# A two-level Strassen matmul with GELU: staging, transposes, split operands and the last outputs rescheduled

## The chip, the core and the metric

One core of a Trainium2 chip (trn2). The metric is the device time of one execution in microseconds (us). Single executions of one kernel spread by several us here. All runs told here count as fast runs (granted clock 0.993 to 1.0 over a whole run). Engines: PE is TensorE (matmul), PEld its weight loads, DVE is VectorE, ACT is ScalarE, POOL is GpSimd, which issues the loads, and SP is SyncE, which issues the stores. PSUM is the memory in which PE accumulates its results.

## The reference

```python
def setup_inputs():
    m, k, n = 4096, 4096, 4096
    return {"a": np.random.randn(m, k).astype(np.float32), "b": np.random.randn(k, n).astype(np.float32)}

def reference(a, b):
    x = np.matmul(a, b)
    return 0.5 * x * (1 + np.tanh(np.sqrt(2 / np.pi) * (x + 0.044715 * x**3)))
```

## The kernel before

A and B are each cut in four quarters. The output is made in 16 blocks ("groups", numbered 0 to 15; four row blocks of A times four column blocks of B), each of which is one tile in every quarter of the output. Seven Strassen products M1 to M7 make a block; block 0 begins with eight plain products, and in blocks 10 to 15 some of the seven are themselves cut by a second Strassen level ("split"). Work is laid out in steps: one step is a quarter of one product, 16 matmuls with 512 columns, 3.45 us. VectorE makes the operand sums (`aS` from A, `bS` from B), the transposes of A (`aT`) and most of the adds of results. ScalarE copies products out of PSUM that are needed again (M5 into `m` or `m5`, M7 into the four buffers `x7`). `bR` is B as loaded; `k_M` and `k_split` are operands of B kept in DRAM, and `bK` is such an operand fetched back; `accX` and `accY` are PSUM.

```python
PRODUCTS = [
    ("M3", "Y", "11", ("12", "22", 1)),          # name, PSUM chain, operand of A, operand of B
    ("M5", "X", ("11", "12", -1), "22"),
    ("M7", "X", ("12", "22", -1), ("21", "22", 1)),
    ("M1", "X", ("11", "22", -1), ("11", "22", -1)),
    ...
]
```

A comes as float32, is cast by the load into one of two `stage` buffers, is transposed by VectorE from there, and is then weighed (squared and summed, for a check of the input's range) by ScalarE in place. The buffer is free for the next load when the weighing is done:

```python
for (quad, h), n in zip(halves, turns(gi)):                 # n: the step of the transpose
    at_step(max(n - LOAD_AHEAD, free_at.pop(0)), load, (load_half, (mb, quad, h)))
    free_at.append(n + 5)
    at_step(n, turn_half, mb, quad, h)
    for x in range(4):                                      # weighed over four steps
        at_step(n + 1 + x, weigh_rows, mb, quad, h, ...)
```

The split products need combined operands of B that are made once, stored to DRAM and fetched for each block. `MAKES` says when: block, product number, step, column block of B, product. Each entry makes five operands, one per step, in the ring `bS` of three buffers, which the sums share:

```python
def make_split(gi, nb, name, p):
    ...
    t = pool.tile([P, 4 * NC], F16, name="bS", tag="bS", bufs=AHEAD + 1)      # AHEAD is 2
    take(t..., o[2], quarter_b(blocks, o[0]), quarter_b(blocks, o[1]))        # VectorE
    keep_operand((nb, "split", s0, k // 2), k % 2, t[:, :])                   # store to DRAM
```

The last block's last output quarter was added up on VectorE, passed through GELU on ScalarE and stored:

```python
elif name == "M6":
    y = post.pop(("x1", i))
    tt(y, X, y, ALU.add)          # VectorE: PSUM + SBUF
    flush()
    waiting.append((gi, i, 1, 1, y, y))   # then ScalarE, then one store of 256 KB
```

## Time and profile before

| | before |
|---|---|
| device time, first 3 runs | 1571.35, 1573.3, 1575.03 us |
| profiled execution | 1571.53 us, span 1570.0 us |
| PE busy | 1547.9 us, 99% of the span |
| VectorE / ScalarE busy | 73% / 38% |
| PE's waits in total | 15.4 us |
| last matmul to the end | 6.65 us |

While its matmuls stay the same, a kernel whose PE is 99% busy can only be improved in the few holes. How the page, PE's waits and its timeline are read for this is shown in the prediction. One more view belongs with them: VectorE's own timeline in block 9, ahead of PE's longest wait (2.79 us, ending at 955.48). Columns: start, duration, engine, line, operation, out<-in, shapes, and in brackets the idle time before it and what ended it.

```profile
937.35 1.22 DVE L933 TENSOR_TENSOR bS<-bK 128x2048 f16<-128x2048 f16 x1
942.29 1.23 DVE L933 TENSOR_TENSOR bS<-bK 128x2048 f16<-128x2048 f16 x1 [3.73 <-DMA k_split<-bS]
...
953.06 1.23 DVE L933 TENSOR_TENSOR bS<-bK 128x2048 f16<-128x2048 f16 x1 [2.92 <-DMA k_split<-bS]
954.20 1.22 DVE L933 TENSOR_TENSOR aS<-aT 128x2048 f16<-128x2048 f16 x1
```

VectorE stands still for 3.73 and 2.92 us (and for 0.85 us in the part left out) until a store of an earlier split operand has landed. The sum `aS` that PE is waiting for stands behind it in VectorE's order, and PE starts 0.06 us after that sum ends (954.20 + 1.22 = 955.42).

### The profile page before, as it was taken

To read this page: it belongs to the slowest core of one execution; us is meant where nothing else is said; L and a number is where in the kernel's file an instruction comes from. 1 tells how busy PE (TensorE), PEld (TensorE's weight loads), DVE (VectorE), ACT (ScalarE), POOL (GpSimd) and SP (SyncE) were. 2 spreads that over 40 slices of the span, in tenths; PEclk is the share of its full clock that TensorE was granted. 3 is DMA by queue.
4 is the path that set the end of the run, shared out by engine and by line. 5 is a ranking of instruction groups with operands and counts; after the bars stand their busy time and mean duration, and the time that the engine had idled before them with its cause. 6 is when DMAs were issued, how large, how long until landed. Compare 5 with 4: busy or idle time off the path is not lost. (4 is left out here: it accounts for less than half of the span.)

```text
span 1570.0 us, 22246 instructions
## 1 busy us (share of the span) xinstructions
PE 1547.9 (99%) x8110; PEld 794.1 (51%) x8110; DVE 1139.6 (73%) x1357; ACT 600.8 (38%) x1322; POOL 462.5 (29%) x830
## 2 busy tenths in 40 slices
PE   9999999999999999999999999999999999999998
PEld 4444444444444444444444443554746457677674
DVE  1598888889778886765557647878749677776774
ACT  5446555465643642211554211121355523232232
POOL 7664433431124311122231222221333312132230
PEclk9999999999999999999999999999999999999999
DMA  9999999994789987799998989898999958688692
GB/s 176 183 224 294 269 304 273 286 216 81 188 220 298 292 299 283 278 416 328 277 283 233 411 317 345 307 414 272 279 263 315 351 156 306 237 283 308 234 332 108
DMA packets 202790, 429.41 MB, mean 274 GB/s; under 512 B 20400, under 2 KB 102320, under 8 KB 200624
## 3 DMA queue, kind: packets, MB, share of 16 engines
q0 software_dynamic: 141472, 265.34, 65.6%
q1 hardware_dynamic: 61200, 162.56, 27.1%
q8 instruction: 66, 1.08, 0.3%
q14 instruction: 52, 0.43, 0.1%
HBM read 340.79 MB, written 162.53 MB: 321 GB/s over the span
## 5 line engine op out<-in xcount | busy, mean ns | idle before, releaser
L468 PEld LDWEIGHTS <-aS 128*128 128x128 f16 x4192 | 410.2, 98 | 510.4 <-issue 7.9
L468 PE MATMUL accX<-bK,aS 128*128 128x512 f16 x1536 | 336.0, 380 | 3.3 <-DVE aS L933 3.3
L933 DVE TENSOR_TENSOR aS<-aT 128x2048 f16<-128x2048 f16 x182 | 217.1, 1219 | 94.7 <-PE accX L468 70.6
L468 PEld LDWEIGHTS <-aT 128*128 128x128 f16 x1600 | 156.6, 98 | 189.2 <-issue 1.4
L919 POOL DMA_DIRECT2D bK<-k_M x236 | 124.8, 534 | 401.5 <-PE accX L468 119.3
L257 POOL DMA_DIRECT2D bR<-in_b_dram x320 | 173.1, 543 | 210.5 <-DMA bR<-in_b_dram 98.2
L271 ACT ACTIVATE stage<-stage 128x512 f16<-128x512 f16 (+1 forms) x320 | 169.5, 532 | 141.0 <-DVE aT L221 108.8
L468 PE MATMUL accY<-bK,aS 128*128 128x512 f16 x896 | 195.0, 379 | 2.2 <-DVE aS L933 1.2
L612 ACT ACTIVATE x<-x 128x512 f32<-128x512 f32 x128 | 78.3, 628 | 251.8 <-DVE x L621 251.7
L468 PE MATMUL accX<-bS,aS 128*128 128x512 f16 x704 | 155.1, 382 | 4.1 <-DVE aS L430 2.5
L430 DVE TENSOR_TENSOR aS<-aT 128x2048 f16<-128x2048 f16 (+1 forms) x112 | 134.0, 1201 | 25.8 <-PE accX L468 14.6
L550 PEld LDWEIGHTS <-aS 128*128 128x128 f16 x1440 | 140.9, 98 | 23.1 <-issue 1.1
L430 DVE TENSOR_TENSOR bS<-bR 128x2048 f16<-128x2048 f16 x110 | 133.5, 1218 | 18.6 <-PE accX L468 13.6
L311 ACT ACTIVATE square<-bR 128x1024 bf16<-128x1024 f16 x120 | 123.1, 1048 | 42.7 <-DVE energy L621 42.0
L257 POOL DMA_DIRECT2D stage<-in_a_dram x144 | 84.5, 593 | 178.8 <-ACT stage L271 106.4
L221 DVE STREAM_TRANSPOSE aT<-stage 128x1024 uint32<-128x1024 uint32 (+1 forms) x61 | 76.0, 1278 | 80.0 <-DMA stage<-in_a_dram 69.5
L579 ACT COPY x<-accX 128x512 f32<-128x512 f32 x116 | 67.8, 586 | 173.0 <-PE accX L468 172.7
L933 DVE TENSOR_TENSOR bS<-bK 128x2048 f16<-128x2048 f16 x70 | 84.3, 1219 | 27.1 <-DMA k_split<-bS 26.9
L621 DVE TENSOR_TENSOR x<-accY,x 128x512 f32<-128x512 f32 x116 | 77.2, 688 | 30.1 <-ACT y L612 20.3
L468 PE MATMUL accY<-bK,aT 128*128 128x512 f16 x448 | 97.8, 379 | 0.0
L468 PE MATMUL accX<-bK,aT 128*128 128x512 f16 x448 | 97.8, 379 | 0.0
L579 ACT COPY m<-accX 128x512 f32<-128x512 f32 x76 | 43.2, 581 | 119.8 <-PE accX L468 95.1
(70 smaller groups left out, 1518.4 us busy)
## 6 DMA issues: line engine op xcount, KB each, us to landing
bK<-k_M POOLq DMA_DIRECT2D x272, 512.0 KB, 10.1
bK<-k_split POOLq DMA_DIRECT2D x90, 512.0 KB, 6.7
bR<-in_b_dram POOLq DMA_DIRECT2D x320, 128.0 KB, 7.4
k_M<-bS SPq DMA_DIRECT2D x80, 512.0 KB, 6.5
k_split<-bS SPq DMA_DIRECT2D x70, 512.0 KB, 7.1
out_dram<-y SPq DMA_DIRECT2D x128, 256.0 KB, 6.3
out_dram<-x SPq DMA_DIRECT2D x128, 256.0 KB, 7.3
stage<-in_a_dram POOLq DMA_DIRECT2D x112, 256.0 KB, 8.4
```

Source lines behind the costliest of these rows:

```text
L221: nc.vector.transpose(dst[:, :, x, :], src)
L257: nc.gpsimd.dma_start(out=dst, in_=src)
L271: nc.scalar.activation(src, src, ACT.Square, accum_out=dst)
L311: nc.scalar.activation(t[:, :], src, ACT.Square)
L430: nc.vector.tensor_tensor(out=x, in0=y, in1=z, op=ALU.add if o[2] > 0 else ALU.subtract)
L468: nc.tensor.matmul(acc[:, :], sa[:, j // 2, i * P : (i + 1) * P, j % 2], sb[:, j, :], start=start and j == 0, stop=stop and j == 3, skip_g ...
L550: nc.tensor.matmul(banks[chain, i][:, :] if wide else out, sa[:, j // 2, r * P : (r + 1) * P, j % 2], sb[:, : NC] if wide else sb[:, j * N ...
L579: nc.scalar.copy(out=t[:, :], in_=src[:, :])
L612: nc.scalar.activation(y[:, :], src[:, :], ACT.Gelu_apprx_tanh)
L621: nc.vector.tensor_tensor(out=o[:, :], in0=x[:, :], in1=y[:, :], op=op)
L919: nc.gpsimd.dma_start(out=dst, in_=kept_unit(*key[1:])[:, x * w : (x + 1) * w])
L933: nc.vector.tensor_tensor(out=t, in0=y, in1=z, op=ALU.add if op > 0 else ALU.subtract)
```

## The change

Its intent: fill PE's holes, each by its own means. The diff, cut to its core:

```diff
-MAKES = ( (6,1,0,1,"M3"), (6,2,1,1,"M5"), (6,3,2,3,"M3"), (6,4,2,3,"M5"), (7,1,3,0,"M2"),
-          (8,2,3,2,"M3"), (8,4,0,2,"M5"), (8,5,3,2,"M1"), (9,2,0,0,"M3"), (9,2,2,0,"M5"),
-          (9,4,2,3,"M1"), (9,5,3,3,"M2"), (10,2,2,2,"M2"), (10,4,0,0,"M1") )
+MAKES = ( (6,0,1,0,"M3"), (6,1,1,1,"M3"), (6,2,1,1,"M5"), (6,3,2,3,"M3"), (7,0,1,2,"M1"),
+          (7,5,3,0,"M2"), (8,2,3,2,"M3"), (8,4,0,2,"M5"), (8,5,3,0,"M5"), (9,1,1,2,"M2"),
+          (9,2,2,3,"M5"), (9,4,0,3,"M1"), (9,5,3,3,"M2"), (10,4,0,0,"M1") )
-SUM_AHEAD = 3      SPLIT_AHEAD = 8      FETCH_AHEAD = 8      LOAD_AHEAD = 7
+SUM_AHEAD = 5      SPLIT_AHEAD = 6      FETCH_AHEAD = 9      LOAD_AHEAD = 9
+RAW_LOAD_AHEAD = 8
+WEIGH_STEPS = 2                       # of the first blocks; the later ones stay at 4
-TURNS = ((2,2), (3,2), (4,2), (5,0), (6,2), (7,3), (9,1), (10,2))
-RAW_TURNS = ((2,2), (3,2), (5,2), (6,1), (7,1), (8,1), (10,1), (11,1))
+TURNS = ((2,2), (3,2), (4,2), (5,0), (6,2), (7,2), (10,1), (10,3))
+RAW_TURNS = ((2,3), (3,3), (5,2), (6,1), (7,1), (8,1), (11,0), (11,0))
-TWO_GROUPS = [x // 2 for x in range(16)] + [8 + 2 * x for x in range(16)]
+TWO_GROUPS = (0,0,1,1,2,2,3,3,4,4,4,4,5,5,5,5,5,7,10,12,14,16,18,18,20,20,24,26,27,27,28,29)
+THIRD = ("22", 1)                     # A22's second half of block 0: four x7 tiles
...
-    (14, "T11_1 W11_1 B11_1a A22_1 B11_1b"),  (16, "T12_1 W12_1:0-4"),  (17, "W12_1:4-16 A21_1"),
+    (14, "T11_1 W11_1 A22_1 B11_1"),          (16, "T12_1"),            (17, "A21_1"),
...  # A22 weighed at steps 18 to 21, A12 at 34 to 49 (before: A12 at 16 and 17, A22 at 34 to 49)
     elif name == "M1":
         m1, x7 = keep("m5", X, 2), post["x7", i]
         tt(x7, x7, m1, ALU.add)
+        if gi == len(groups) - 1:
+            x1 = post.pop(("x1", i))
+            tt(X, X, x1, ALU.add)
...
+    elif gi == len(groups) - 1:       # M6 of the last block
+        flush()
+        if i < RT - 1:
+            emit(gi, i, 1, 1, new_y(), X)
+            return
+        ...
+        for x, queue in enumerate((nc.sync, nc.scalar)):
+            y = new_y()
+            nc.scalar.activation(y[:, :w], X[:, x * w : (x + 1) * w], ACT.Gelu_apprx_tanh)
+            queue.dma_start(out=out[...], in_=y[:, :w])
...
-                at(gi, s, 2 * c, keep_raw, nb, name, ob, c)
+                at(gi, s + 2 * (gi == 1 and name == "M5"), 2 * c, keep_raw, nb, name, ob, c)
```

More of the change, by code (lines that the diff above doesn't have):

```diff
@@ L69 @@
 MAKES = (
-    (6, 1, 0, 1, "M3"),
+    (6, 0, 1, 0, "M3"),
+    (6, 1, 1, 1, "M3"),
     (6, 2, 1, 1, "M5"),
     (6, 3, 2, 3, "M3"),
-    (6, 4, 2, 3, "M5"),
-    (7, 1, 3, 0, "M2"),
+    (7, 0, 1, 2, "M1"),
+    (7, 5, 3, 0, "M2"),
     (8, 2, 3, 2, "M3"),
     (8, 4, 0, 2, "M5"),
-    (8, 5, 3, 2, "M1"),
-    (9, 2, 0, 0, "M3"),
-    (9, 2, 2, 0, "M5"),
-    (9, 4, 2, 3, "M1"),
+    (8, 5, 3, 0, "M5"),
+    (9, 1, 1, 2, "M2"),
+    (9, 2, 2, 3, "M5"),
+    (9, 4, 0, 3, "M1"),
     (9, 5, 3, 3, "M2"),
-    (10, 2, 2, 2, "M2"),
     (10, 4, 0, 0, "M1"),
@@ L86 @@
 STAY_AHEAD = 19
-SUM_AHEAD = 3
+SUM_AHEAD = 5
 BLOCK_AHEAD = 12
-SPLIT_AHEAD = 8
-FETCH_AHEAD = 8
+SPLIT_AHEAD = 6
+FETCH_AHEAD = 9
 SPLITS = {M3_M5: (10, 11, 12, 13, 14, 15), M2_M1: (13, 14, 15)}
-LOAD_AHEAD = 7
-TURNS = ((2, 2), (3, 2), (4, 2), (5, 0), (6, 2), (7, 3), (9, 1), (10, 2))
-RAW_TURNS = ((2, 2), (3, 2), (5, 2), (6, 1), (7, 1), (8, 1), (10, 1), (11, 1))
+RAW_LOAD_AHEAD = 8
+WEIGH_STEPS = 2
+LOAD_AHEAD = 9
+TURNS = ((2, 2), (3, 2), (4, 2), (5, 0), (6, 2), (7, 2), (10, 1), (10, 3))
+RAW_TURNS = ((2, 3), (3, 3), (5, 2), (6, 1), (7, 1), (8, 1), (11, 0), (11, 0))
 PLAIN = [
@@ L104 @@
 N_PLAIN = 2 * len(PLAIN)
-TWO_GROUPS = [x // 2 for x in range(16)] + [8 + 2 * x for x in range(16)]
+TWO_GROUPS = (0, 0, 1, 1, 2, 2, 3, 3, 4, 4, 4, 4, 5, 5, 5, 5, 5, 7, 10, 12, 14, 16, 18, 18, 20, 20, 24, 26, 27, 27, 28, 29)
 C21_FIRST = (0, 5, QPH - 1)
+THIRD = ("22", 1)
 N_WARM = 46
@@ L199, in load_a @@
         x0 = (ih * MH + mb * TM) // Q + x
+        if (quad, c) == THIRD:
+            tiles = staged[mb, quad, c] = staged.get((mb, quad, c), [])
+            ts = []
+            for i in range(x // (NX // RT), (x + n) // (NX // RT)):
+                t = pool.tile([P, NC], F32, name="x7", tag="x7", bufs=RT).bitcast(F16)
+                tiles.append(t.rearrange("p (x r) -> p x r", r=RUN))
+                ts += [
+                    (
+                        tiles[i][g * Q : (g + 1) * Q, :, :],
+                        a_v[kh, g, :, x0 - x + i * NX // RT : x0 - x + (i + 1) * NX // RT, c * RUN : (c + 1) * RUN],
+                    )
+                    for g in range(4)
+                ]
+            return ts
         if not h:
@@ L215, in turn_a @@
         if mb:
-            src = staged[mb, quad, h].rearrange("p x (c r) -> p c x r", c=CH)[:, c]
-        else:
-            src = staged[mb, quad, c][:, x, :]
-        src = src.bitcast(U32).rearrange("p mb (jj q) -> p jj mb q", q=Q)
+            parts = [(x, staged[mb, quad, h].rearrange("p x (c r) -> p c x r", c=CH)[:, c])]
+        elif (quad, c) == THIRD:
+            n = NX // RT
+            parts = [
+                (slice(i * n, (i + 1) * n), staged[mb, quad, c][i]) for i in range(x.start // n, x.stop // n)
+            ]
+        else:
+            parts = [(x, staged[mb, quad, c][:, x, :])]
         dst = a_tiles[mb, quad, c].bitcast(U32).rearrange("p jj (mb q) -> p jj mb q", q=Q)
-        nc.vector.transpose(dst[:, :, x, :], src)
+        for x, src in parts:
+            src = src.bitcast(U32).rearrange("p mb (jj q) -> p jj mb q", q=Q)
+            nc.vector.transpose(dst[:, :, x, :], src)
     def load_half(mb, quad, h):
@@ L292, in weigh_first @@
             k = ((kh * CH + c) * 2 + ih) * NX + x
-            weigh_row(stats["a"][:, k : k + 1], staged[0, quad, c][:, x, :])
+            n = NX // RT
+            row = staged[0, quad, c][x // n][:, x % n, :] if (quad, c) == THIRD else staged[0, quad, c][:, x, :]
+            weigh_row(stats["a"][:, k : k + 1], row)
     def weigh_first_half():
@@ L682, in settle_fresh @@
             waiting.append((gi, i, 0, 0, y, y))
-        elif name == "M6":
+        elif gi == len(groups) - 1:
[3 more added lines that the diff above has]
+                return
+            mb, nb = groups[gi]
+            r0, c0, w = MH + mb * TM + i * P, NH + nb * NC, NC // 2
+            for x, queue in enumerate((nc.sync, nc.scalar)):
+                y = new_y()
+                nc.scalar.activation(y[:, :w], X[:, x * w : (x + 1) * w], ACT.Gelu_apprx_tanh)
+                queue.dma_start(out=out[r0 : r0 + P, c0 + x * w : c0 + (x + 1) * w], in_=y[:, :w])
+        else:
             y = post.pop(("x1", i))
@@ L727, in half_path @@
         (9, "T22_0 W22_0 A12_1+B21_1a B21_1b"),
-        (14, "T11_1 W11_1 B11_1a A22_1 B11_1b"),
-        (16, "T12_1 W12_1:0-4"),
-        (17, "W12_1:4-16 A21_1"),
-        (18, "S2 S3 T22_1"),
-        (23, "T21_1"),
-        (34, "W22_1:0-1"),
-        (35, "W22_1:1-2"),
-        (36, "W22_1:2-3"),
-        (37, "W22_1:3-4"),
-        (38, "W22_1:4-5"),
-        (39, "W22_1:5-6"),
-        (40, "W22_1:6-7"),
-        (41, "W22_1:7-8"),
-        (42, "W22_1:8-9"),
-        (43, "W22_1:9-10"),
-        (44, "W22_1:10-11"),
-        (45, "W22_1:11-12"),
-        (46, "W22_1:12-13"),
-        (47, "W22_1:13-14"),
-        (48, "W22_1:14-15"),
-        (49, "W22_1:15-16"),
+        (14, "T11_1 W11_1 A22_1 B11_1"),
+        (16, "T12_1"),
+        (17, "A21_1"),
+        (18, "S2 S3 T22_1 W22_1:0-4"),
+        (19, "W22_1:4-8"),
+        (20, "W22_1:8-12"),
+        (21, "W22_1:12-16"),
+        (23, "T21_1"),
+        (34, "W12_1:0-1"),
+        (35, "W12_1:1-2"),
+        (36, "W12_1:2-3"),
+        (37, "W12_1:3-4"),
+        (38, "W12_1:4-5"),
+        (39, "W12_1:5-6"),
+        (40, "W12_1:6-7"),
+        (41, "W12_1:7-8"),
+        (42, "W12_1:8-9"),
+        (43, "W12_1:9-10"),
+        (44, "W12_1:10-11"),
+        (45, "W12_1:11-12"),
+        (46, "W12_1:12-13"),
+        (47, "W12_1:13-14"),
+        (48, "W12_1:14-15"),
+        (49, "W12_1:15-16"),
         (50, "W21_1:0-1"),
@@ L828, in half_path @@
         for (quad, h), n in zip(halves, turns(gi)):
-            at_step(max(n - LOAD_AHEAD, free_at.pop(0)), load, (load_half, (mb, quad, h)))
-            free_at.append(n + 5)
+            at_step(max(n - (LOAD_AHEAD if gi >= N_RAW else RAW_LOAD_AHEAD), free_at.pop(0)), load, (load_half, (mb, quad, h)))
+            slow = WEIGH_STEPS if gi < N_RAW else 4
+            free_at.append(n + slow + 1)
             at_step(n, turn_half, mb, quad, h)
-            for x in range(4):
-                at_step(n + 1 + x, weigh_rows, mb, quad, h, list(range(NX // 2))[x * NX // 2 // 4 : (x + 1) * NX // 2 // 4])
+            for x in range(slow):
+                at_step(n + 1 + x, weigh_rows, mb, quad, h, range(x * NX // 2 // slow, (x + 1) * NX // 2 // slow))
             if h and quad in ("12", "21"):
-                at_step(n + 5, weigh_half, mb, int(quad[0]) - 1)
+                at_step(n + slow + 1, weigh_half, mb, int(quad[0]) - 1)
     for nb, gi in last_raw.items():
```

## The prediction

> **What bounds the kernel now.** I read the page first: is there one engine that sets the time?
>
> ```profile
> span 1570.0 us, 22246 instructions
> PE 1547.9 (99%) x8110; PEld 794.1 (51%) x8110; DVE 1139.6 (73%) x1357; ACT 600.8 (38%) x1322; POOL 462.5 (29%) x830
> PEclk9999999999999999999999999999999999999999
> DMA  9999999994789987799998989898999958688692
> ```
>
> TensorE (PE) is busy in 99% of the span. No part of the change takes a matmul away: the list of split operands has 14 entries before and after, and the order of products is the same. So everything but PE's holes is fixed, and the question is how large the holes are. The DMA row matters too: 16 engines nearly full means that a transfer started late also lands late. Second view: what PE itself waits for, over the whole span.
>
> ```profile
> PE accX L468 <- DVE aS L430: 5.0, 4, 2.0
> PE accX L468 <- DVE aS L933: 3.3, 2, 2.8
> PE accX L468 <- ACT m L579: 1.5, 1, 1.5
> PE accY L468 <- DVE x L621: 1.4, 2, 1.0
> PE accX L480 <- DVE table L1158: 1.4, 1, 1.4
> PE accY L468 <- DVE aS L933: 1.2, 1, 1.2
> PE accX L550 <- DVE x L621: 0.9, 1, 0.9
> PE accY L499 <- DMA bR<-in_b_dram: 0.5, 1, 0.5
> PE accX L468 <- DVE bS L430: 0.2, 1, 0.2
> ```
>
> Columns: total us, times, longest. They sum to 15.4 us in 14 waits; 1.4 of it is the start. Third view, PE's timeline, says where they lie and shows two hidden costs.
>
> ```profile
> 85.79 0.61 PE L468 MATMUL accX<-bS,aS 128*128 128x512 f16 x2 [0.55 <-DVE aS L430]
> 88.40 15.24 PE L468 MATMUL accX<-bS,aS 128*128 128x512 f16 x62 [2.00 <-DVE aS L430]
> ...
> 440.58 3.63 PE L468 MATMUL accX<-bR,aS 128*128 128x512 f16 x16 [1.97 <-DVE aS L430]
> ...
> 487.70 13.98 PE L468 MATMUL accY<-bR,aS 128*128 128x512 f16 x64
> 501.52 13.98 PE L468 MATMUL accY<-bS,aS 128*128 128x512 f16 x64
> ...
> 949.06 3.63 PE L468 MATMUL accX<-bK,aS 128*128 128x512 f16 x16 [0.54 <-DVE aS L933]
> 955.48 8.77 PE L468 MATMUL accX<-bK,aS 128*128 128x512 f16 x32 [2.79 <-DVE aS L933]
> ```
>
> Undisturbed, 64 matmuls take 13.82 us to the next start (487.70 to 501.52), 0.216 us each, though the row says 13.98: each pipeline drain costs 0.16 us, which a wait adds to the idle time shown. And 62 matmuls should take 62 x 0.216 + 0.16 = 13.6 us, but took 15.24; 32 should take 7.1, but took 8.77. Just after the two longest starvations about 1.7 us more is lost. Fourth view, engine use by stretch, says why (columns: length, busy us of PE, PEld, DVE, ACT, POOL, then granted clock, DMA, GB/s):
>
> ```profile
> 88.00:91.00 3.00, 2.60 (x8) 0.98 (x9) 2.89 (x6) 1.17 (x2) 1.99 (x4) 0.65 1.39 188
> ...
> 955.00:959.00 4.00, 3.52 (x10) 1.32 (x11) 3.48 (x4) 0.00 (x0) 1.05 (x2) 0.61 1.02 417
> ```
>
> The clock had dropped. So the loss is 15.4 - 1.4 = 14.0 us of waits, plus 13 x 0.16 = 2.1 of drains, plus 2 x 1.7 = 3.4 of slow clock: 19.5 us. By place (the kernel goes through 16 blocks of output, 0 to 15, about 97 us each):
> - block 0: 0.45 at 35 us, 0.44 at 72, 0.45 at 78, then 0.55 and 2.00 at 86 and 88 with the slow clock: 6.4 in all, of which 4.6 belong to the last two;
> - block 4: 1.97, 1.52 and 0.23 at 441, 447 and 484: 4.2;
> - blocks 7 and 9: 1.19 at 752; 0.54 and 2.79 with slow clock at 949 and 955; 1.00 at 993: 1.4 + 5.3 + 1.2 = 7.9;
> - block 12: 0.9 at 1201: 1.05.
> After the last matmul (end 1563.35) there are 6.65 us of tail.
>
> **What the Trainium skill says.** "TensorE: Matmul & The Clock Gate", Part 1, has the array's clock fall to half after an idle window of about 3.4 us, free-running, so that a shorter hole can or can't trip it. The trace agrees: after holes of 2.0 and 2.8 us starts are spaced about twice as far for some 3.4 us, while the pair at 441 and 447 (1.97, 1.52) cost no clock. A stall near 2 us or more may thus cost 1.7 more. "DMA: Bandwidth & Descriptors", section "Issuing engines are not separate DMA queues", says that all issuers share the same 16 DMA engines; here stores of split operands take a median 7.1 us to land, loads of A 8.4 us. The same page, "Anatomy of one DMA", puts about 2 us of fixed cost on a DMA, most of it the receipt; the last store here is issued at 1564.75 and moves its data only from about 1565.9, which fits. "PSUM — Partial Sum Buffer", "The four PSUM rules", says that a VectorE write leaves the accumulate bits alone and that a later matmul adds onto it where the bit is set, which the new last block relies on; the old kernel's split joins do the same.
>
> **The change part by part.**
>
> *A22's second half of block 0, third place.* Before, its staging buffer is the one A11's second half occupies until weighed, and it queues behind half of B11's loads. VectorE shows it: the transpose at 83.76 waits 2.25 us for its load, the second at 86.37 follows, then sums until 88.9, when PE resumes. Now it goes into the four x7 buffers, free in block 0, and ahead of B11's eight loads. In the issuing order it gains the four B11 issues of 72.74 to 75.86, about 3.5 us. The transposes then come near 80.3 and 83, the last sum near 85.4; the product starts at 85.1 with its first half. The 4.6 us go, but its weighing must now finish before x7 is needed: 16 rows at 0.40 us, eight of them on ScalarE before its copies of M5, which gate the next product. Rows from 81.5 to 84.7, first copy done 85.3: 0.2 to 0.8 us of new wait. The three small waits before stay (0.6 each). Net gain 3.8.
>
> *A on another plan.* In block 4 VectorE idles 7.2 us for a staged load and transposes at 436.45 what was due at about 431.5; PE then waits 1.97, and ScalarE, with weighing and squares queued, is late with M5's copies (1.52). Rows were weighed over 4 steps, so a buffer came free 5 steps after its transpose; with 2 steps it comes after 3. This load can go at step 28 counted from block 3's first, not 30: 2 x 3.45 = 6.9 us earlier, against about 5 us of lateness. Squares of B are moved out of these steps as well. Against it: both halves of A21 now turn in the same step of M4 (4 transposes, 4.7 us, not 2.4, before 5.4 us of sums of M1's results), where 0.23 was lost already. Gain 4.2 less about 0.7: 3.5.
>
> *Split operands singly.* In block 9 two lists of five overlap in three steps, two operands a step, in a ring of three buffers whose stores take 7 us: three per 7 us is all the ring passes, and a step is 3.45 us. VectorE waits for these stores, in blocks 7 to 9:
>
> ```profile
> DVE bS L933 <- DMA k_split<-bS: 19.9, 9, 5.7
> ```
>
> The sums PE needs stand behind them in order. New entries never overlap (two steps lie between the two lists in the second half of block 9), and the list of block 7 leaves the steps where A is transposed. One operand per 3.45 us needs a buffer for 7.1 us out of 10.4: the ring holds. Also five operands rather than six are made for a block column not being multiplied, 2 MB less to fetch of 429. Gain 7.9 less about 0.9 for stores that land late in a full DMA: 7.0.
>
> *Last outputs from PSUM.* M1's partial sum is added into PSUM one product earlier (4 x 0.69 us of VectorE, hidden under 13.8 us of matmuls), so the last chain loses one VectorE step of 0.70 us, and the last tile goes out as two halves on two queues: 128 KB lands some 0.4 us sooner than 256. Gain 1.0.
>
> *B22 kept later, sums up to 5 steps ahead, loads 9 steps ahead.* No PE wait of its own to take away; cushions. Block 12's 1.05 us comes after 25 us in which VectorE is never idle; one transpose moves nearer to it (the sixth half is due earlier), sums may move away. Net 0.
>
> Sum: 3.8 + 3.5 + 7.0 + 1.0 = 15.3. For a wait in a place that I don't see I take off 1.3: 14.0. 1573.3 - 14.0 = **1559.3 us**.
>
> **The rivals.**
> - *All holes close*: 1573.3 - 19.5 - 1.0 = 1552.8. Against it: the three early waits of block 0 (together 1.8) hang on loads that the change leaves in place. Practically the floor.
> - *The wait turns into another one.* VectorE is 85 of 97 us busy in blocks 1 to 3, and a burst shifts to another step: the double turn of A21, or the early copies held by the weighing in block 0. Two new holes near 2 us, one with a slow clock, give back 6 us: 1565.
> - *The DMA is the true limit.* The page gives the two queues 65.6% and 27.1% of the engines' time; earlier loads push stores and fetches back: only the tail, block 0 and part of block 9 are gained, 7 us: 1566. Against it: the table by stretch shows nothing moved from 390 to 400 us, just when loads of A wait for buffers, so earlier issue fills holes.
> - *Slower*: would need over 31 us of new PE waits, twice all there are now.
>
> **Range and chances.** Single runs spread from 1571.35 to 1575.03, some 2 us either side, so the floor of 1552.8 and the second and third rivals set the range: 1554 to 1566. Faster by over 2% is below 1541.8, under the floor: 0.01. Slower by over 2%: 0.01. Within 2%: 0.98.
>
> **What would show it.** Right, step by step: no wait of PE for aS at 85 to 89 and the granted clock at 1.0 there; no PE wait near 430 to 450; VectorE's wait for split stores down from 26.9 us over the whole span to under 8, and no hole in blocks 7 and 9; last matmul near 1550, tail 5.6 us. PE's waits in total should be 3 to 6 us, not 15.4, with PE's busy time near 1543 (slow stretches and drains gone). Wrong: a wait for ScalarE's copies at 85 us; a wait for bS or aS near 480 or 1200; stores of split operands that still stop VectorE; or another stretch of lower clock.

## The result, and the profile after

| | before | after |
|---|---|---|
| device time, median (range, runs) | 1572.32 us (1568.32 to 1575.03, 4) | 1556.16 us (1553.08 to 1559.46, 4) |
| ratio, 95% interval | | 0.99, 0.9866 to 0.9934 |
| profiled execution, span | 1570.0 us | 1557.8 us |

A ratio is the mean time of one kernel's fast runs over the mean of the other's of the same rounds, so it is not quite the ratio of the medians beside it. The result is 3.1 us below the point predicted and inside its range. The page of the changed kernel:

```profile
span 1557.8 us, 22302 instructions
PE 1544.9 (99%) x8110; PEld 794.2 (51%) x8110; DVE 1139.1 (73%) x1359; ACT 600.9 (39%) x1323; POOL 462.3 (30%) x830
```

Same matmuls, 12.2 us less span. What PE waits for (columns as before: total us, times, longest):

```profile
PE accX L575 <- DVE x L646: 3.8, 1, 3.8
PE accX L505 <- DVE table L1201: 1.4, 1, 1.4
PE accX L493 <- ACT m L604: 1.0, 2, 0.6
PE accX L493 <- DVE aS L455: 0.5, 1, 0.5
PE accY L493 <- DVE bS L455: 0.4, 1, 0.4
PE accY L493 <- DVE x L646: 0.2, 1, 0.2
```

The sum is 7.3 us instead of 15.4. The waits for `aS` at L933 of before (its name here is L976) and those of block 4 are gone; one new wait of 3.8 us for adds of results is now more than half of the rest. It stands at 1188.58 us, at the start of block 12, and the clock falls behind it (columns: length, busy us of PE, PEld, DVE, ACT, POOL, granted clock, DMA share, GB/s):

```profile
1188.00:1192.00 4.00, 3.42 (x17) 2.16 (x17) 3.80 (x8) 4.00 (x12) 0.00 (x0) 0.57 1.02 365
```

To compare many profiles I worked one number per place out of each trace: for every pair of successive matmuls, the time between their starts less the undisturbed 0.216 us (0.109 for 256 columns), counted where the excess is over 0.06 us. That takes in the wait, the drained pipeline and the slow clock. Block 0 is counted from 30 us on; the start before that loses 1.7 to 2.8 us in kernels of either kind and is left out. By block, in us, with the tail from the last matmul's end to the end of the span; every run but the first and the ninth is told of below:

```
run                      block 0    1-3      4    7-9  10-11     12   total   tail    span
before                       6.4    0.0    4.4    7.8    0.0    1.1    19.7   6.65  1570.0
before_again                 4.5    0.0    3.7    9.2    0.0    4.3    21.7   6.81  1571.9
tail_only                    2.0    0.0    4.5    7.6    0.0    4.2    18.3   5.55  1567.4
makes_only                   5.6    0.0    4.1    0.0    0.0    0.0     9.7   6.32  1559.0
old_makes_plan               3.6    0.4    0.0    6.0    0.0    4.5    14.5   5.83  1563.7
old_makes                    3.7    1.4    0.0    4.4    0.0    0.0     9.5   5.59  1557.8
old_weigh                    4.4    0.0    4.4    0.0    0.0    7.1    15.8   5.74  1564.7
no_third                     3.3    0.0    0.0    0.0    0.0    2.2     5.5   5.59  1553.7
after                        3.0    0.3    0.0    0.0    0.0    5.3     8.6   5.56  1557.8
after_again                  3.5    0.7    0.0    0.0    0.0    6.6    10.7   5.74  1559.8
old_turns                    4.0    0.0    0.0    0.0    0.0    8.9    12.9   5.48  1561.5
weigh2all                    3.4    0.0    0.0    0.0    0.0    6.2     9.6   5.53  1558.1
turn51                       2.8    1.8    0.0    0.0    0.0    0.4     5.0   5.57  1553.6
turn51_early_keep            4.4    8.3    0.0    0.0    0.0    0.3    13.0   5.55  1561.7
```

The check on this table: span less total less tail is 1543.6 for before, 1543.6 for after, and 1542.6 to 1543.5 for all the others. So nothing but these places moves the time by more than the 1 us by which the start differs. Blocks left out of the table lose 0.1 us at most. "Blocks 7-9" holds 705 to 1000 us, where an old plan's lost time lies.

### The profile page after: what moved, and what is told of

The parts are those of the page before. It is cut to its first block, busy times and chain, and to the rows that moved or that the text cites. A ratio compares the mean times of both kernels' runs of the same rounds, so it can differ in the third digit from the quotient of the medians.

```text
span 1557.8 us, 22302 instructions
## 1 busy us (share of the span) xinstructions
PE 1544.9 (99%) x8110; PEld 794.2 (51%) x8110; DVE 1139.1 (73%) x1359; ACT 600.9 (39%) x1323; POOL 462.3 (30%) x830
## 5 line engine op out<-in xcount | busy, mean ns | idle before, releaser
L976 DVE TENSOR_TENSOR aS<-aT 128x2048 f16<-128x2048 f16 x182 | 217.4, 1219 | 93.9 <-PE accX L493 61.7
L962 POOL DMA_DIRECT2D bK<-k_M x228 | 120.6, 533 | 419.5 <-PE accX L493 117.9
L294 ACT ACTIVATE stage<-stage 128x512 f16<-128x512 f16 (+1 forms) x304 | 163.0, 538 | 108.3 <-DVE aT L244 80.6
L575 PEld LDWEIGHTS <-aS 128*128 128x128 f16 x1440 | 141.4, 98 | 26.9 <-issue 4.5
L244 DVE STREAM_TRANSPOSE aT<-stage 128x1024 uint32<-128x1024 uint32 (+1 forms) x59 | 73.4, 1277 | 72.0 <-DMA stage<-in_a_dram 62.9
L280 POOL DMA_DIRECT2D stage<-in_a_dram x136 | 80.0, 595 | 138.8 <-ACT stage L294 104.1
L976 DVE TENSOR_TENSOR bS<-bK 128x2048 f16<-128x2048 f16 x70 | 84.3, 1216 | 27.8 <-DMA k_split<-bS 27.6
```

The costliest lines, as they stand in the source:

```text
L244: nc.vector.transpose(dst[:, :, x, :], src)
L280: nc.gpsimd.dma_start(out=dst, in_=src)
L294: nc.scalar.activation(src, src, ACT.Square, accum_out=dst)
L575: nc.tensor.matmul(banks[chain, i][:, :] if wide else out, sa[:, j // 2, r * P : (r + 1) * P, j % 2], sb[:, : NC] if wide else sb[:, j * N ...
L962: nc.gpsimd.dma_start(out=dst, in_=kept_unit(*key[1:])[:, x * w : (x + 1) * w])
L976: nc.vector.tensor_tensor(out=t, in0=y, in1=z, op=ALU.add if op > 0 else ALU.subtract)
```

## The experiments

My theory is the prediction's: each part closes its own hole. The rivals: a hole was closed by another part, or the wait turned into another one, or a hole of the first profile was chance. First group, on one chip: what is the new wait in block 12?

**after_again: the changed kernel, unaltered.** (No edit.)

> The changed kernel unaltered. Its four runs so far lie in two pairs, 1553 and 1559 us; the profiled one of the slow pair has a single PE wait of 3.8 us at the start of block 12 (1188 us) with a slow clock after it, about 5.4 us in all. Theory: that wait is the difference of the pairs, because a load of A lands late in a crowded DMA and VectorE starts its backlog late. Expected: median 1553 to 1560, and a profile whose time beside 1559.46 goes with the size of the wait in block 12: about 1554 if it is under 1 us. Rival: the two pairs are two chips, and then all runs here agree within 2 us whatever block 12 does.

Measured: median 1555.9 us, six runs from 1553.71 to 1563.58, ratio 0.991 (0.9876 to 0.9944). The profiled run, 1561.41, again has the wait of 3.8 us in block 12 and loses 6.6 us there. Runs on one chip spread over 9.9 us, so the rival of two chips falls. That the quick runs are those without the wait is likely from the sizes, but the unprofiled runs left no trace, so it isn't shown.

The chain behind the wait, on VectorE in the profile of the changed kernel, from block 11 to block 12:

```profile
1159.25 2.37 DVE L244 STREAM_TRANSPOSE aT<-stage 128x1024 uint32<-128x1024 uint32 x2 [11.33 <-DMA stage<-in_a_dram]
1161.55 0.65 DVE L646 TENSOR_TENSOR x<-x,x 128x512 f32<-128x512 f32 x1
...
1184.27 2.46 DVE L646 TENSOR_TENSOR x<-x,accY 128x512 f32<-128x512 f32 x4
1186.66 2.47 DVE L646 TENSOR_TENSOR x<-accY,x 128x512 f32<-128x512 f32 x4
```

VectorE idles 11.33 us for a load of A. The adds of M1's results (from 1161.55) stand behind the transpose, though their data has been there since PE left M1 at 1151.6. From there VectorE works without a pause, and the adds of block 11's last results, which free PSUM for block 12, end at 1189. That a later instruction can't pass a waiting one is what the Trainium skill says in "PSUM — Partial Sum Buffer", section "Engine vs sequencer instructions": the queues of ScalarE, VectorE and GpSimd are strictly first in, first out. This trace agrees: 11.33 us idle with 5.4 us of adds ready.

**turn51: that one transpose a step later, behind the adds.**

```diff
-TURNS = (..., (4, 2), (5, 0), (6, 2), ...
+TURNS = (..., (4, 2), (5, 1), (6, 2), ...
```

> Only the fourth transpose of a coming block of A is put one step later (fifth product, second quarter instead of first), so that VectorE adds up M1's results (8 adds, 5.4 us) before it waits for the load. Theory (the late load of A holds VectorE in order, and the adds behind it are what PE waits for in block 12): the wait at block 12 goes under 1 us, 2 to 5 us faster than the unaltered kernel where that has the wait. Rival (VectorE has simply too much to do between 1160 and 1190 us): no gain, the wait stays above 2 us.

Measured: median 1555.1 us (1554.07 to 1561.18, 6 runs; five of them within 1554.07 and 1555.35), ratio 0.9905 (0.9873 to 0.9937). Block 12 loses 0.4 us in its profile:

```profile
1150.44 0.69 DVE L646 TENSOR_TENSOR x<-x,x 128x512 f32<-128x512 f32 x1 [0.96 <-ACT x L604]
...
1159.25 2.38 DVE L244 STREAM_TRANSPOSE aT<-stage 128x1024 uint32<-128x1024 uint32 x2 [3.19 <-DMA stage<-in_a_dram]
```

The load lands no sooner, the transpose starts at the same 1159.25, but the adds were done meanwhile, and VectorE's wait is 3.19 us instead of 11.33. The theory of order holds in the trace; the rival of sheer load falls. As a time the gain isn't clear: the interval of its ratio overlaps that of the unaltered kernel nearly whole.

**weigh2all: the later blocks of A weighed in 2 steps too.**

```diff
-            slow = WEIGH_STEPS if gi < N_RAW else 4
+            slow = WEIGH_STEPS
```

> The later blocks of A are weighed in 2 steps as the first ones are, not 4, so staging buffers come free 2 steps (6.9 us) sooner. Theory of the late load: the transposes in block 11 and 15's neighbours no longer wait 11 to 12 us for their loads, block 12's wait goes under 1 us, 2 to 5 us faster. Rival (DMA is full there, an earlier issue lands no sooner): the same time, the transposes wait as before.

Measured: median 1559.55 us (1553.91 to 1561.28), ratio 0.9921 (0.9889 to 0.9953); block 12 loses 6.2 us. My theory missed: VectorE's wait for loads of A is 66.8 us in total, against 62.9 in the changed kernel. But the edit hardly tests the rival. The four loads behind the late transpose are issued from 1139.83 us on, not from 1141.10: 1.3 us sooner, not 6.9; the profile puts GpSimd's waits just before them down to earlier transfers. What the trace shows is a slow landing: between 1110 and 1165 us loads of A take a median of 13.8 us from issue to landing, and 13.6 in the changed kernel. Whether a load issued 6.9 us sooner would land sooner stays open.

**old_turns: the later transposes at their old times.**

```diff
-TURNS = ((2,2), (3,2), (4,2), (5,0), (6,2), (7,2), (10,1), (10,3))
+TURNS = ((2,2), (3,2), (4,2), (5,0), (6,2), (7,3), (9,1), (10,2))
```

> The changed kernel with the old times of the transposes of A in the later blocks (sixth half one step later, last two spread otherwise). My prediction had the sixth half's earlier place add 2.4 us of VectorE work just where block 12 stalls. If that is the cause, block 12's wait falls to about 1 us as in the kernel before and the time by 2 to 4 us; if the late fourth load is the cause, the wait stays at 2 to 4 us and the time is the same within 1.5 us.

Measured: median 1557.24 us (1554.06 to 1563.07), ratio 0.9913 (0.9881 to 0.9945); block 12 loses 8.9 us. So the sixth half's earlier place, which the prediction named as a danger for block 12, isn't the cause. The fourth transpose, ahead of the adds in both plans, is.

Second group, on one chip: the changed kernel with one part undone each.

**no_third: A22's second half of block 0 staged as before.**

```diff
-THIRD = ("22", 1)
+THIRD = None
... and the lines of steps 14 to 49 as in the kernel before
```

> The changed kernel without the third place: A22's second half of block 0 in the two staging buffers, the loads of B11 around it and the weighing of A12 and A22 as in the kernel before. Theory of the prediction: the wait of PE for the sums of A22 at 83 to 90 us comes back with its slow clock: 4 to 4.6 us lost there instead of 1 to 2, and the time rises by 3 to 4 us. Rival (the later squares and loads of the new plan alone freed block 0): no more than 2 us lost there.

Measured: median 1557.08 us (1555.07 to 1561.35, 4 runs), ratio 0.9932 (0.9898 to 0.9966). Block 0 loses 3.3 us, and PE's wait for the sums of A22 is 0.7 us. My theory missed by its whole size.

**old_weigh: the first blocks of A on the old plan.**

```diff
-WEIGH_STEPS = 2    RAW_LOAD_AHEAD = 8    RAW_TURNS and TWO_GROUPS of the changed kernel
+WEIGH_STEPS = 4    RAW_LOAD_AHEAD = 7    RAW_TURNS and TWO_GROUPS of the kernel before
```

> The changed kernel with the first blocks' A weighed in 4 steps, transposed, loaded and the squares of B placed as before. Theory: PE's waits in block 4 (430 to 485 us) come back, 3.5 to 4.5 us lost there, none elsewhere. Rival (they came from earlier holes or from ScalarE's load by chance): under 1 us there.

Measured: median 1563.28 us (1558.55 to 1566.28), ratio 0.9953 (0.9919 to 0.9987). PE's waits between 414 and 512 us are back, to the tenth:

```profile
PE accX L493 <- DVE aS L455: 2.0, 1, 2.0
PE accX L493 <- ACT m L604: 1.5, 1, 1.5
```

The same question to the changed kernel has an empty answer. Block 4 loses 4.4 us, as in the kernel before. On VectorE the wait for loads of A near 405 to 450 us is 10.7 us in the kernel before and with this edit, and 1.7 in the changed one. The transpose that came too late, in the kernel before and then in the changed one:

```profile
436.45 2.37 DVE L221 STREAM_TRANSPOSE aT<-stage 128x1024 uint32<-128x1024 uint32 x2 [7.23 <-DMA stage<-in_a_dram]
```

```profile
424.32 2.37 DVE L244 STREAM_TRANSPOSE aT<-stage 128x1024 uint32<-128x1024 uint32 x2 [1.69 <-DMA stage<-in_a_dram]
```

Its load waits for the end of a weighing on ScalarE and is issued at 409.64 us in the changed kernel and at 416.66 with this edit, 7.0 us later (the prediction has 6.9). The theory holds for the plan as a whole; the edit sets back four things at once (steps of the weighing, distance of the loads, transposes, squares of B), and which of them is needed I haven't separated.

**old_makes: the old list of split operands, the new distances.**

```diff
-MAKES of the changed kernel
+MAKES of the kernel before
```

> The changed kernel with the old list of split operands alone, so that in block 9 two are made in one step; sums up to 5 steps ahead and loads 9 ahead stay. Theory of the prediction (stores of the ring of three buffers): VectorE waits for stores of split operands about as long as before (27 us; but the changed kernel has 27.6 too, which already speaks against my figure of under 8), and 4 to 6 us are lost at 940 to 955 us. Rival: the sums made up to 5 steps ahead cover VectorE's waits, and then PE loses under 1.5 us in blocks 7 and 9 although the list is the old one.

Measured: median 1559.8 us (1558.92 to 1563.32), ratio 0.9948 (0.9916 to 0.9979). Blocks 7 to 9 lose 4.4 us, at the same places as before (743, 941 to 951, 982 us), with no slow clock this time. So sums made further ahead don't cover the old list by themselves; the list is needed.

**old_makes_plan: the later blocks' whole plan undone.**

```diff
-MAKES, TURNS of the changed kernel; SUM_AHEAD 5, SPLIT_AHEAD 6, FETCH_AHEAD 9, LOAD_AHEAD 9
+MAKES, TURNS of the kernel before;  SUM_AHEAD 3, SPLIT_AHEAD 8, FETCH_AHEAD 8, LOAD_AHEAD 7
```

> The old list, and with it the old distances (sums 3 steps ahead, split sums 8, fetches 8, loads 7) and transposes of the later blocks: all of the later blocks' plan undone. Both theories expect about 6 to 8 us lost in blocks 7 and 9, as in the kernel before; block 12 then tells whether its wait of 4 us and more belongs to the new plan (about 1 us here) or comes and goes with the loads of A in either plan.

Measured: median 1565.65 us (1562.92 to 1566.22), ratio 0.9974 (0.9944 to 1.0005). Blocks 7 to 9 lose 6.0 us, block 12 loses 4.5. So block 12's wait also occurs under the old plan: it comes and goes with a load's landing.

Third group, on one chip: the kernel before again, and with one part of the change.

**before_again: the kernel before, unaltered.** (No edit.)

> The kernel before, unaltered, for a second profile of it. Taking the third place out of the changed kernel did not bring back the wait at block 0, so that wait may be a thing of the one profile of before. Theory A (chance): block 0 loses 2 to 3.5 us here between 30 and 125 us, not the 6.4 of the first profile, while block 4 (about 4.4), blocks 7 and 9 (about 7.9) and the tail (6.65) come out as before. Theory B (the new plan's loads of later blocks also free block 0, or old waits are fixed): 5 us or more again. Ratio 1.00 either way.

Measured: median 1570.38 us (1562.97 to 1575.66, 6 runs), ratio 0.9985 (0.9949 to 1.002). Blocks 4 and 7 to 9 (3.7 and 9.2 us) and the tail (6.81) come out much as before; block 0 loses 4.5 us instead of 6.4, between my two theories. Five profiles without the third place lose 6.4, 4.5, 2.0, 5.6 and 3.3 us in block 0, mean 4.4; the nine with it lose 2.8 to 4.4, mean 3.6. So the place is worth about 0.7 us, not 3.8, which is less than the spread of the five: that it gains anything in all isn't shown. The first profile was the unluckiest of five.

Why it isn't worth more shows in engine use by stretch (columns as above), first before_again, then turn51, one of the nine with the third place:

```profile
90.00:100.00 10.00, 10.00 (x48) 4.56 (x47) 10.00 (x11) 5.89 (x10) 6.53 (x13) 1.00 1.25 215
...
110.00:120.00 10.00, 9.88 (x47) 4.41 (x45) 10.00 (x13) 0.00 (x0) 5.90 (x12) 1.00 1.17 230
```

```profile
90.00:100.00 10.00, 10.00 (x48) 4.48 (x46) 10.00 (x11) 5.68 (x11) 5.43 (x10) 1.00 1.28 229
...
110.00:120.00 10.00, 8.54 (x40) 3.72 (x39) 10.00 (x14) 1.79 (x3) 5.65 (x11) 1.00 1.19 229
```

The third busy figure is VectorE: 10.00 of 10 us in both. From 90 to 120 us VectorE is the bound (9.86 us from 100 to 110). PE arrives earlier with A22's sums on time and then waits for VectorE between 110 and 120 us (8.54 us busy of 10). In turn51 PE loses 0.4 us at 83 and 1.8 at 111 to 116; in no_third, 1.4 at 84 and 0.3 at 116. All 14 profiles fit this: between 79 and 92 us those without the third place lose 1.4 to 4.4 us (mean 3.0) and those with it 0.4 to 2.0 (mean 1.0); between 92 and 124 us it is 0.0 to 0.3 (mean 0.2) without it and 1.0 to 1.9 (mean 1.6) with it, under the old plan for A (old_weigh) as under the new one. About 2.0 us are gained and 1.4 given back. The wait has been moved.

**makes_only: the kernel before with the new list of split operands.**

```diff
-MAKES of the kernel before
+MAKES of the changed kernel
```

> The kernel before with the new list of split operands alone (distances, transposes, A plan, tail as before). Theory of single making: blocks 7 and 9 lose under 3 us instead of 7.9, 5 to 7 us faster, ratio about 0.996; the wait for stores stays near 27 us over the span but leaves block 9. Rival: without sums made 5 steps ahead the new list just moves its holes to block 7, where the stores now wait: 4 us or more lost there. Block 0 is as in the kernel before: a third look at it (2 to 3.5 us if the first was chance).

Measured: median 1560.07 us (1558.66 to 1564.67, 6 runs) beside 1571.54 of the kernel before in the same rounds, ratio 0.9931 (0.99 to 0.9961). Blocks 7 to 9 lose nothing. This one table of 14 entries is the larger part of the whole gain, and the rival falls. It beat my 5 to 7 us; part of that is block 12, which happens to lose nothing in its profile. The wait for stores, on VectorE over the whole span, doesn't fall: 27.1 us, as I expected by then. How that can be is told in the next section.

**tail_only: the kernel before with the new end.**

```diff
+        if gi == len(groups) - 1:            # in M1
+            x1 = post.pop(("x1", i))
+            tt(X, X, x1, ALU.add)
...
+    elif gi == len(groups) - 1:              # M6 as in the changed kernel
```

> The kernel before with the new last block's end alone (M1's sum into PSUM earlier, last tile in two halves on two queues). Expected: from the last matmul to the end 5.6 us, not 6.65; time about 1 us less, too little to show in the times (the interval is wider). All else as before: blocks 4, 7 and 9 lose what they lost, and block 0 is looked at a fourth time. Rival: the second queue costs its own start-up and the tail stays above 6.3.

Measured: from the last matmul to the end 5.55 us, against 6.65, 6.81 and 6.32 in the three profiles with the old end (mean 6.59) and 5.48 to 5.83 in all eleven with the new. The time, 1568.73 us (1563.38 to 1572.74), ratio 0.9978 (0.9946 to 1.0011), can't show 1 us. The rival falls. The last instructions before and after, where the last matmul ends at 1563.35 and at 1552.27 us:

```profile
1563.37 0.69 DVE L621 TENSOR_TENSOR x<-accX,x 128x512 f32<-128x512 f32 x1 [0.17 <-PE accX L468]
1564.09 0.63 ACT L612 ACTIVATE x<-x 128x512 f32<-128x512 f32 x1 [0.23 <-DVE x L621]
```

```profile
1552.35 0.66 ACT L720 ACTIVATE y<-accX 128x256 f32<-128x256 f32 x2 [0.27 <-PEq L1231]
1552.76 0.33 SPq L721 DMA_DIRECT2D out_dram<-y  x1
1553.04 0.38 ACTq L721 DMA_DIRECT2D out_dram<-y  x1
```

VectorE's 0.69 us has left the chain, and the first half's store is issued (1552.76) before the second half's GELU is through. The last store is issued 0.78 us after the last matmul instead of 1.42. The halves do not land sooner, though: 3.6 and 3.5 us after their issue, against a median of 3.2 for the last four whole stores before. What is left of the 1.0 us lies behind the last landing: 2.2 us pass from there to the end in the first two profiles with the old end, 1.4 in the third (makes_only) and 1.3 to 1.4 with the new one. I have no explanation for that part.

**turn51_early_keep: turn51 with B22 of block 1 stored where it was before.**

```diff
-                at(gi, s + 2 * (gi == 1 and name == "M5"), 2 * c, keep_raw, nb, name, ob, c)
+                at(gi, s, 2 * c, keep_raw, nb, name, ob, c)
```

> The version with the fourth transpose a step later, and with B22 of block 1 kept where the kernel before kept it. Theory: block 12 loses under 1 us again, time as for that version, 1555. The later keeping of B22: if it is needed, PE waits appear in blocks 1 and 2 (124 to 318 us), 1 us or more for sums of B; if it is a cushion only, as I predicted, blocks 1 and 2 lose under 0.7 us, which is less than the 1.8 us lost at 251 us with the later keeping and the later transpose.

Measured: median 1564.32 us (1563.08 to 1569.63, 6 runs), ratio 0.9961 (0.993 to 0.9992). Block 12 loses 0.3 us, the second profile of the later transpose without a wait there. But blocks 1 to 3 lose 8.3 us, 7.7 of it in one wait of PE and the slow clock after it (0.59 from 162 to 167 us), behind a wait of VectorE for loads of B:

```profile
PE accX L493 <- DVE bS L455: 6.0, 1, 6.0
...
DVE bS L455 <- DMA bR<-in_b_dram: 10.1, 2, 7.5
```

In this run the two stores of B22, 1 MB each, are issued at 131.7 us, while B's loads for block 1 are still coming; in turn51 they go at 163 and 169 us. The later keeping, which I had put down as worth nothing, is worth 6.5 us in these two profiles (8.3 against turn51's 1.8 us in blocks 1 to 3); the median is 9.2 us above turn51's, and the two ranges don't overlap. The kernel before keeps B22 early and loses nothing there; which other part makes the later keeping needed I haven't separated.

No version clearly beats the changed kernel. turn51 has the lowest median of the runs made in its group and closes block 12 in two profiles of two, counting the last run; its time is the same within the noise.

## Why the prediction was right or wrong, point by point

**The bound, and the sum of the holes: right.** The 19.5 us of the prediction are 19.7 in the table; the changed kernel's profile loses 8.6, and the tail accounts for the other 1.1 us of the 12.2. PE's waits were predicted at 3 to 6 us in total and are 7.3, because of block 12.

**A on another plan, 3.5 us: right, a little more.** The kernels with the old plan lose 3.7 to 4.5 us in block 4, every kernel with the new plan 0.0. The double transpose of A21, for which I took off 0.7, cost nothing.

**Split operands singly, 7.0 us: right in size, wrong in one step.** Kernels with the old list and old distances lose 6.0 to 9.2 us in blocks 7 to 9, those with the new list 0.0. The step that failed is "the ring holds", with VectorE's wait for split stores under 8 us. It was 26.9 us before and is 27.6 after (2.3 more stand at `aS`, which shares the ring). Between 902 and 1000 us it fell from 16.1 us to 1.3, plus those 2.3; between 709 and 806 us, block 7, it rose from 3.0 to 10.7. VectorE runs ahead of PE in block 7 and fills the ring before PE's pace asks for it:

```profile
705.41 2.35 DVE L976 TENSOR_TENSOR bS<-bK 128x2048 f16<-128x2048 f16 x2
714.77 1.22 DVE L976 TENSOR_TENSOR bS<-bK 128x2048 f16<-128x2048 f16 x1 [7.00 <-DMA k_split<-bS]
...
718.67 1.23 DVE L976 TENSOR_TENSOR aS<-aT 128x2048 f16<-128x2048 f16 x1 [0.25 <-PE accX L493]
```

These lines are VectorE's in block 7 of the changed kernel. It waits 7.00 us for a store, and soon after it waits for PE to free a buffer: it is still ahead, and PE loses nothing. In block 9 of the kernel before, waits of 3.73, 0.85 and 2.92 us one after the other stopped PE. (The fetches fell from 272 of 512 KB to 264, 4.2 MB read less, where I had counted 2.) So the change left the sum of these waits as it was and took them from a place where PE's sums stood behind them to one where nothing did.

**A22's third place, 3.8 us: the mechanism seen, the gain wrong.** A22's transposes came at 79.4 to 83.6 us, near the predicted 80.3 and 83, and the copies of M5 held by the weighing cost two waits of 0.6 and 0.4 us (predicted 0.2 to 0.8). But the term was taken as the whole 4.6 us of one profile, which was the largest of five, and what PE gained it lost again behind VectorE, fully busy from 90 to 120 us. Net, about 0.7 us, not clear of the spread. The rival "the wait turns into another one" is what happened here.

**Last outputs from PSUM, 1.0 us: right in size, wrong in one step.** 6.59 us to 5.61, as means of three and eleven profiles. VectorE's step left the chain as predicted, and the last store is issued 0.64 us sooner. The step that failed is that a half "lands some 0.4 us sooner": the halves took 3.6 and 3.5 us, whole stores 3.2. In two of the three old profiles the rest came after the last landing, so part of the full 1.0 us is unexplained.

**Block 12, net 0: wrong.** The changed kernel's two profiles lose 5.3 and 6.6 us there, the kernel before's 1.1 and 4.3. I had blamed 25 us of uninterrupted VectorE work and a transpose moving nearer; the runs show a late load of A at the head of VectorE's order, and adds that could have gone first. Over all the profiles with the transpose ahead of the adds, what block 12 loses goes with how late that transpose begins, counted from PE's start on M4, when M1's results are complete:

```
run              transpose late by, us     block 12 loses, us
old_makes                -0.8                     0.0
makes_only                0.2                     0.0
before                    2.5                     1.1
tail_only                 4.0                     4.2
before_again              4.1                     4.3
no_third                  5.9                     2.2
old_makes_plan            6.1                     4.5
weigh2all                 6.6                     6.2
after                     7.7                     5.3
after_again                8.8                     6.6
old_weigh                 9.2                     7.1
old_turns                10.7                     8.9
```

Where list and distances are both old it is 2.5 to 6.1 us late, where both are new 5.9 to 10.7 us. In turn51, with the adds first, a transpose 7.0 us late goes with only 0.4 us lost. Which transfers push that load back I haven't separated: the new distances with the old list (old_makes) and the old distances with the new list (makes_only) both had it in time, in one profile each.

**B22 kept later, net 0: wrong for this kernel.** Taking it back in turn51 raises the loss in blocks 1 to 3 from 1.8 to 8.3 us. It gains nothing over the kernel before, but the new plan needs it, as far as one variant shows.

**The sum.** Predicted 14.0 us off. The medians differ by 16.2 us here and by 14.9 in the first group of experiments; the profiled executions by 12.2. One term was 3.1 us too large (A22), two together some 1.5 too small (A's plan and single making), and block 12 took about 3 more in the profiles; the 1.3 set aside for an unseen wait stood against that. They came out near the mark. In that the point was lucky; the range was not.

## What to carry to other kernels

When one engine is 99% busy, work out the lost time by place from its own start times, and check that span less losses is the same for every version: then each part of a change can be judged at its place, though the total spreads by 10 us from run to run. Take several profiles before explaining a hole of a few us; one that depends on when a transfer lands varied here from 2.0 to 6.4 us. And ask of a wait not how long it is but what stands behind it in that engine's order: moving a transpose behind adds that are ready removed the wait, where the attempt to make its data come earlier did not.

## What the Trainium skill lacked or had wrong

- "TensorE: Matmul & The Clock Gate", Part 1, gives an idle window of about 3.4 us for the fall of the clock. Shorter holes tripped it here: 2.79 us at 955 us (clock 0.61 after it), and 0.55 and 2.00 us close together at 86 and 88 us (0.65); longer ones of 2.94 us in before_again (at 793 us) and 3.03 us in old_makes_plan (at 1195 us) did not (clock 1.00 after both). The prediction's "near 2 us or more" is no rule either, then: the length of the hole alone doesn't decide. The page says that the window is free-running, but not how little work within it counts as idle.
- "DMA: Bandwidth & Descriptors", "Anatomy of one DMA", fits 2.0 us plus the bytes over 436e3 per us for a DMA that GpSimd issues; for 512 KB, an estimate from that page's formula, this is 3.2 us. Fetches of that size, which GpSimd issues, took a median of 10.1 us (`k_M`) and 6.7 us (`k_split`) from issue to landing in the kernel before, with 93% of the 16 engines' time used. SyncE's stores of 256 KB of results took a median of 7.3 us (`x`) over the whole span and 3.2 us at its very end. The page gives a latency of the HBM under high load, but no figure for the landing of a whole transfer, which is what sets the distance a load or store must be issued ahead.
- "Perfetto Trace Analysis", "Optimization Strategy", says to find the gaps of the contended engine and what blocks it. It lacks the caution that the total wait of a helper engine need not show what the contended engine loses: with 26.9 us of VectorE's waits for stores PE lost 5.3 us behind them in block 9, with 27.6 us nothing in blocks 7 to 9.
- No page says how far a trace of one kernel differs from its next: four profiles lost 2.0 to 6.4 us in block 0, with the same instructions there.
